# RWKV-7 chunk matrices stored as 64 columns instead of a 128-column block diagonal, in a fused two-block kernel

## The chip, the cores and the metric

The kernel runs on one core of one Trainium2 chip. The metric is the device time of one execution in microseconds (us). The core has a TensorE (PE, matrix products; PEld is its weight load), a VectorE (DVE), a ScalarE (ACT), a GpSimd (POOL) and a SyncE (SP) that issues the DMAs. Each works through its own instructions in a fixed order and waits for the others by semaphores.

## The reference, cut to what matters

A first transformer block (differential and stick-breaking attention, cross attention, an MLP) is followed by a second one: latent attention (MLA) and RWKV-7 side by side, their outputs joined and multiplied by `w_o`, then a product-key expert layer (PEER). The part that changes is RWKV-7: 8 heads of width 64 over 256 tokens, in the reference a recurrence.

```python
def rwkv7_step(state, inp):
    r_t, w_t, k_t, v_t, kk_t, a_t = inp
    sk = jnp.einsum('bhij,bhj->bhi', state, kk_t)
    state = (state * w_t[:, :, None, :]
             - sk[..., None] * (kk_t * a_t)[:, :, None, :]
             + v_t[..., None] * k_t[:, :, None, :])
    y = jnp.einsum('bhij,bhj->bhi', state, r_t)
    return state, y
...
x = x + jnp.concatenate([y_a, y_b], axis=-1) @ w_o[l]   # y_a from MLA, y_b from RWKV-7
x = x + peer_ffn(rms_norm_2(x, g_ffn[l]), w_pq[l], sub_keys[l], expert_u[l], expert_v[l])
```

## The kernel before, in words

RWKV-7 is computed in chunks of 64 tokens. There are four chunks; 128 partitions hold two of them, so an array has an index `t` (which pair) and the two chunks `c` of a pair lie in the partition halves `par(0)` and `par(1)`. The eight heads go in two groups: the generator `r0` does heads 0 to 3, `r1` heads 4 to 7. For each group, pair and head the kernel

- forms the masked chunk matrices AB and KB (products at L1147, in quarters of the PE array; masks on DVE at L1155). AB and KB have 128 columns: both chunks' 64x64 blocks on a diagonal, zeros elsewhere;
- inverts the 16x16 diagonal blocks of a triangular matrix. They go to DRAM and back (L1165, L1167), are inverted on DVE in many small steps (L1176 to L1191), and go out and back again (L1193, L1196) into the zeroed array `p21` that holds Z and X;
- finishes the solve by products of 128x128 matrices with a step on DVE or ACT after each: KB times v (L1214), A0 times X (L1226), Q times Z (L1233), Z times KR (L1242), A0 times Q (L1249), Z times KR again (L1258), which gives KU;
- forms the part of the output that a chunk makes by itself (L1268, L1308), the states from chunk to chunk (L1282, L1285, L1289, then the chain L1299), and adds states times receptance (L1314). The chunk's output is normalised (L1325 to L1336) and written to the tiles `y2[2]` and `y2[3]`.

A float32 product is two MATMUL records in the trace, a float32r product one; so eight records of L1226 are four products.

MLA is the third generator, `mla()`. For each pair of heads it projects queries and keys (L339 to L341), computes scores (L1399, L1400), a softmax on DVE and ACT (L1402 to L1415), transposes (L1421, tiles `me` and `mpT`), outputs (L1432) and their norm (L1435, L1436, L1440), and writes `y2[0]` or `y2[1]` (L676, L677). `w_o` reads all four y2 tiles (L351, L352, L354 and L339 to L341), its weights being split into a high and a low part (`lo`, L332). After it comes `w_pq`, the first product of PEER (tile `xs`).

A scheduler orders the instructions of every engine ahead of time by its own estimates; the code gives priorities:

```python
prio = {r0: R0_PRIO, m_: MLA_PRIO, r1: R1_PRIO}     # 100, 200, 100
...
with tc.high_priority(offset=prio[it]):
    end = next(it, done) is done
```

PSUM has eight banks: `plin()` hands out four (`lin`, used by MLA and the linear layers), `pw(g)` two for each group (`w`).

Of the kernel before, what the change touches and what calls it, by code (L numbers as in the profile page):

```python
# [20 lines left out]
P = 128  # L21
# [17 lines left out]
KB_POOL = 0  # L39
# [86 lines left out]
def _consts():  # L126
# [9 lines left out]
    same = i[:, None] // 64 == i[None, :] // 64  # L136
    items.append(("sT", (same & (i[:, None] < i[None, :])).astype(f)))
    items.append(("iT", (same & (i[:, None] <= i[None, :])).astype(f)))
    for b in (16,):
        m = (i[:, None] // (2 * b) == i[None, :] // (2 * b)) & (i[:, None] // b < i[None, :] // b)  # L140
        items.append((f"m{b}", m.T.astype(f)))
# [74 lines left out]
def body(tc, A, out):  # L216
# [3 lines left out]
    with es:  # L220
# [815 lines left out]
        CDEC = math.exp(-0.5)  # L1036
        rst = ml.tile([P, T], F32, tag="me", name="rst")
# [25 lines left out]
        def rwkv(g):  # L1063
# [72 lines left out]
            yield  # L1136
            if g == 0:
                AB, KB = (st.tile([P, 2, 4, 2, P], F32, name=n) for n in ("AB0", "KB0"))
            else:
                AB, KB = xslot("AB", 2, [2, 4, 2, P])  # L1140
            for dst, lh in ((AB, beta), (KB, khat)):
                for t in range(2):
                    ps = [pw(g), pw(g)]
                    for i in range(2):
                        for pr_, c in ((0, 0), (1, 1), (0, 1), (1, 0)):
                            rs, ts = par(pr_), slice(t * P + c * 64, t * P + c * 64 + 64)
                            PE.matmul(ps[pr_][par(c), i * P:i * P + P].rearrange("p (a s) -> p a s", a=2), lhsT=lh[rs, i, ts],  # L1147
                                      rhs=kr[rs, i, :, ts], start=i == 0, stop=i == 1, skip_group_check=True)
                    for pr_ in range(2):
                        bc = [P, 2, 2, 2, 64]  # L1150
                        o_ = dst[:, t, pr_:4:2].rearrange("p h a (c s) -> p h a c s", c=2)
                        s_ = ps[pr_][:, :T].rearrange("p (h a s) -> p h a s", h=2, a=2)[:, :, :, None].to_broadcast(bc)
                        m_ = m2.rearrange("p a (c s) -> p a c s", c=2)[:, None].to_broadcast(bc)
                        if dst is AB or not KB_POOL:
                            V.tensor_tensor(o_, s_, m_, op=OP.mult)  # L1155
                        else:
                            S.activation(o_, s_, AF.Copy)
                            G.tensor_tensor(o_, o_, m_, op=OP.mult)
                if dst is AB:
# [13 lines left out]
            G.memset(p21, 0.0)  # L1173
# [45 lines left out]
            z4 = lambda p: p.rearrange("p a b (c t) -> p (a b) c t", c=2).rearrange("p a c t -> p (a c) t").rearrange(  # L1219
                "p (t h) s -> p t h s", t=2)  # L1220
            Z, X, Q = z4(p1), z4(p2), z4(p3)
            mk = C("m16")[:, None].to_broadcast([P, 4, P])
            for t in range(2):
                p_ = pw(g)
                for i in range(4):
                    PE.matmul(p_[:, i * P:i * P + P], lhsT=AB[:, t, i, 0], rhs=X[:, t, i], start=i == 0, stop=i == 3,  # L1226
                              skip_group_check=True)
                V.tensor_tensor(Q[:, t], f3(p_), mk, op=OP.mult)
            yield
            for t in range(2):  # L1230
                p_ = pw(g)
                for i in range(4):
                    PE.matmul(p_[:, i * P:i * P + P], lhsT=Q[:, t, i], rhs=Z[:, t, i], start=i == 0, stop=i == 3,  # L1233
                              skip_group_check=True)
                V.tensor_tensor(Z[:, t], Z[:, t], f3(p_), op=OP.subtract)
# [3 lines left out]
            for t in range(2):  # L1239
                p_ = pw(g)  # L1240
                for i in range(4):
                    PE.matmul(p_[:, i * P:i * P + P], lhsT=Z[:, t, i], rhs=KR[:, t, i], start=i == 0, stop=i == 3,  # L1242
                              skip_group_check=True)
                S.activation(Q[:, t], f3(p_), AF.Copy, scale=inv[:, 2:3])
            yield
            for t in range(2):
                p_ = pw(g)
                for i in range(4):
                    PE.matmul(p_[:, i * P:i * P + P], lhsT=AB[:, t, i, 0], rhs=Q[:, t, i], start=i == 0, stop=i == 3,  # L1249
                              skip_group_check=True)  # L1250
                V.scalar_tensor_tensor(hd(KR[:, t]), f3(p_), inv[:, 3:4], hd(KR[:, t]), op0=OP.mult, op1=OP.add)
            yield

            KU = KB[:, :, :, 0].rearrange("p t h (a d) -> p t h a d", a=2)
            for t in range(2):
                p_ = pw(g)
                for i in range(4):
                    PE.matmul(p_[:, i * P:i * P + P], lhsT=Z[:, t, i], rhs=KR[:, t, i], start=i == 0, stop=i == 3,  # L1258
                              skip_group_check=True)
                S.activation(KB[:, t, :, 0], f3(p_), AF.Copy, scale=-1.0)  # L1260
            yield

            rt = kr[:, :, 1]
            p_ = pw(g)
            for t in range(2):
                for h in range(4):
                    o_ = (2 * t + h // 2) * P
                    PE.matmul(p_[par(h), o_:o_ + P], lhsT=KU[:, t, h, 0], rhs=AB[:, t, h, 1], start=t == 0 and h < 2,  # L1268
                              stop=t == 1 and h > 1, skip_group_check=True)
            sj = lambda a: a.rearrange("p j (t s) -> p j t s", t=2)  # L1270
            V.tensor_tensor(sj(rt), p_.rearrange("p (t j s) -> p j t s", t=2, j=2), sj(rt), op=OP.add)
# [7 lines left out]
            for c in (1, 0, 2):  # L1279
                t, cs = c // 2, slice((c % 2) * 64, (c % 2) * 64 + 64)  # L1280
                for rs, o_, h64, h in hh:
                    PE.matmul(pn[c][rs, o_], lhsT=kt[cs, t, h64], rhs=vt[cs, t, h64], start=c < 2 and h < 2, stop=False,  # L1282
                              skip_group_check=True)
                for rs, o_, h64, h in hh:
                    PE.matmul(pn[c][rs, o_], lhsT=bt[cs, t, h64], rhs=KU[cs, t, h, 1], start=False, stop=False,  # L1285
                              skip_group_check=True)
                if c > 0:
                    for rs, o_, h64, h in hh:
                        PE.matmul(pm[c][rs, o_], lhsT=KU[cs, t, h, 0], rhs=bt[cs, t, h64], start=False, stop=False,  # L1289
                                  skip_group_check=True)  # L1290
            ld = lambda c: lend[:, :, c:c + 1].to_broadcast([P, 2, 64])
            V.tensor_tensor(N[:, 0], pj(pn[0]), ld(0), op=OP.mult)
            for c in (1, 2):
                V.tensor_tensor(M[:, c], pj(pm[c]), C("id2")[:, None].to_broadcast([P, 2, 64]), op=OP.add)
            yield
# [7 lines left out]
            p_ = pw(g)  # L1303
            for t in range(2):
                for i in range(2):
                    for h in range(4):
                        rs, o_, h64 = par(h), (2 * t + h // 2) * P, slice(h * 64, h * 64 + 64)
                        PE.matmul(p_[rs, o_:o_ + P], lhsT=KU[:, t, h, 1] if i else vt[:, t, h64],  # L1308
                                  rhs=(AB if i else KB)[:, t, h, 1], start=t + i == 0 and h < 2, stop=False,
                                  skip_group_check=True)  # L1310
            for c in range(1, 4):
                for h in range(4):
                    rs, o_ = par(h), (2 * (c // 2) + h // 2) * P + (c % 2) * 64
                    PE.matmul(p_[rs, o_:o_ + 64], lhsT=N[rs, c - 1, h // 2], rhs=rt[rs, h // 2, c * 64:c * 64 + 64],  # L1314
                              start=False, stop=c == 3 and h > 1, skip_group_check=True)

            Yc, sq, rr_ = p1[:, 0], p1[:, 1], p2[:, 0]
            jt = lambda a: a.rearrange("p j (t s) -> p t j s", t=2)
            pt = p_.rearrange("p (t j s) -> p t j s", t=2, j=2)
# [210 lines left out]
        done = object()  # L1530
# [307 lines left out]
```

## Time and profile before

| | |
|---|---|
| time of 3 runs, us | 1448.38, 1449.96 (median), 1451.75 |
| the profiled execution, us | 1447.91 |
| its span in the trace, us | 1446.1 |
| granted TensorE clock, mean | 0.993 |
| PE busy | 1414.1 us, 98% |
| DVE, ACT, POOL busy | 1087.6, 793.6, 147.3 us |
| second group's block inversion on DVE | 541.6 to 560.0 us |
| second group's first product at L1226 | 569.49 us |
| first product of w_pq | 641.13 us |

The span is what the profiler saw of one execution; 1.8 us lie around it. All positions below are us from the start of the span. RWKV's chunk work and MLA lie between about 500 and 641 us; what stands before and behind that is the same program in both kernels.

### The profile page before, as it was taken

The numbers are of one execution on the slowest core, as the hardware profiler recorded it, in microseconds if no ns is written. First come the engines' busy times: TensorE is split into PE (matmuls) and PEld (weight loads), VectorE is DVE, ScalarE is ACT, GpSimd is POOL, SyncE is SP. The second block draws the span as 40 slices with busy tenths as digits, with TensorE's granted clock in tenths as the row PEclk, the third lists the DMA queues.
The fourth block names the chain that finished last, engine by engine and source line by source line (L and its number), as shares of the span: only waits on it lengthen the run. The fifth ranks groups of instructions, "written<-read, shape, count | busy, mean of one in ns | idle before, by whom it ended". The sixth has DMA issues, their size and how long they took to land.

```text
span 1446.1 us, 24458 instructions
## 1 busy us (share of the span) xinstructions
PE 1414.1 (98%) x9262; PEld 1248.9 (86%) x9262; DVE 1087.6 (75%) x1986; ACT 793.6 (55%) x1334; POOL 147.3 (10%) x159
## 2 busy tenths in 40 slices
PE   8999999999999888999999999999999999999998
PEld 7888999888888866899999988888888888888887
DVE  7876676886659988579999789899996555555554
ACT  6856655555557445554545566555555444444443
POOL 6500101000114443220000000000000000000000
PEclk9999999999999998999999999999999999999999
DMA  6543445566664411155565555556556566666664
GB/s 220 176 149 104 142 146 155 183 190 201 197 197 148 144 45 27 38 150 190 162 189 175 178 180 158 170 152 176 157 175 199 191 191 195 195 190 193 197 192 146
DMA packets 75911, 237.36 MB, mean 164 GB/s; under 512 B 14608, under 2 KB 17808, under 8 KB 75792
## 3 DMA queue, kind: packets, MB, share of 16 engines
q1 hardware_dynamic: 75792, 235.79, 53.1%
q8 instruction: 73, 1.20, 0.3%
q14 instruction: 46, 0.38, 0.1%
HBM read 233.27 MB, written 2.49 MB: 163 GB/s over the span
## 4 chain that ended last, share of the span: by engine, by line
PE 89%; DVE 7%; DMA 2%; ACT 1%; issue 1%; SPq 0%; DVEq 0%; ACTq 0%
PE lin L348 19%; PE lin L354 17%; PE w L1818 8%; PE w L1815 8%; PE w L1814 8%; PE lin L351 7%; PE lin L352 7%; PE w L1725 2%; DVE lo L332 2%; PE lin L500 1%; PE lin L502 1%; PE lin L501 1%; PE w L1639 0%; ACT hi L330 0%; DMA raw<-w_o 0%
## 5 line engine op out<-in xcount | busy, mean ns | idle before, releaser
L332 DVE TENSOR_TENSOR lo<-raw,hi 128x1024 fp32r<-128x1024 f32 (+1 forms) x432 | 530.7, 1229 | 249.1 <-PE w L1815 92.2
L330 ACT ACTIVATE hi<-raw 128x1024 fp32r<-128x1024 f32 x437 | 458.9, 1050 | 408.9 <-DMA raw<-eu 112.6
L1815 PE MATMUL w<-lo,wh 128*128 128x512 f32 x504 | 155.3, 389 | 0.0
L1818 PE MATMUL w<-hi,wl 128*128 128x512 f32 x504 | 155.2, 389 | 0.0
L348 PE MATMUL lin<-hbh,hi 128*128 128x512 f32 x344 | 135.5, 394 | 0.0
L348 PE MATMUL lin<-hbl,hi 128*128 128x512 f32 x344 | 135.1, 393 | 0.0
L1814 PE MATMUL w<-hi,wh 128*128 128x512 f32 x504 | 134.8, 389 | 0.0
L354 PE MATMUL lin<-hbh,lo 128*128 128x256 f32 x512 | 129.7, 286 | 0.7 <-DVE lo L332 0.7
L354 PE MATMUL lin<-hbl,lo 128*128 128x256 f32 x512 | 127.9, 283 | 0.0
L1818 PEld LDWEIGHTS w<-hi,wl 128*128 128x128 f32 x504 | 94.6, 188 | 19.7
L1814 PEld LDWEIGHTS w<-hi,wh 128*128 128x128 f32 x504 | 94.5, 188 | 19.6
L1815 PEld LDWEIGHTS w<-lo,wh 128*128 128x128 f32 x504 | 94.5, 188 | 19.5
L354 PEld LDWEIGHTS lin<-hbh,lo 128*128 128x128 f32 x512 | 97.3, 190 | 3.5 <-DVE lo L332 1.1
L354 PEld LDWEIGHTS lin<-hbl,lo 128*128 128x128 f32 x512 | 97.7, 191 | 2.6
L1797 ACT ACTIVATE wh<-GA 128x512 fp32r<-128x512 f32 x64 | 40.5, 634 | 73.8 <-PE w L1815 73.8
L348 PEld LDWEIGHTS lin<-hbl,hi 128*128 128x128 f32 x344 | 64.9, 189 | 10.9
L348 PEld LDWEIGHTS lin<-hbh,hi 128*128 128x128 f32 x344 | 64.9, 189 | 10.6
L546 POOL TENSOR_TENSOR sqa<-sqa,sq 128x256 f32<-128x256 f32 x37 | 34.9, 945 | 314.6 <-ACT sq L542 299.8
L348 PE MATMUL lin<-a,hi 128*128 128x512 f32 x256 | 64.8, 395 | 0.0
L348 PE MATMUL lin<-xs,hi 128*128 128x512 f32 x256 | 63.3, 392 | 0.0
L354 PE MATMUL lin<-xs,lo 128*128 128x256 f32 x384 | 53.8, 285 | 0.0
L348 PEld LDWEIGHTS lin<-xs,hi 128*128 128x128 f32 x256 | 46.4, 189 | 8.5
(597 smaller groups left out, 3073.8 us busy)
## 6 DMA issues: line engine op xcount, KB each, us to landing
raw<-eu SPq DMA_DIRECT2D x128, 512.0 KB, 3.7
raw<-ev SPq DMA_DIRECT2D x128, 512.0 KB, 4.2
raw<-w_up SPq DMA_DIRECT2D x32, 512.0 KB, 3.6
raw<-w_down SPq DMA_DIRECT2D x32, 512.0 KB, 4.5
raw<-w_in SPq DMA_DIRECT2D x20, 512.0 KB, 3.7
raw<-w_in_s SPq DMA_DIRECT2D x16, 512.0 KB, 4.9
raw<-w_pq SPq DMA_DIRECT2D x16, 512.0 KB, 3.6
raw<-w_in_m SPq DMA_DIRECT2D x8, 512.0 KB, 3.7
```

Of the source, the lines that this page charges most:

```text
L330: S.activation(hi[:, :n], raw[:, :n], AF.Copy)
L332: eng.tensor_tensor(lo[:, :n], raw[:, :n], hi.bitcast(F32)[:, :n], op=OP.subtract)
L348: PE.matmul(ps.rearrange("p (a t) -> p a t", a=2), lhsT=wh[:, o], rhs=x.both[:, c], start=at, stop=False, skip_group_check=True)
L351: PE.matmul(ps[:, :T], lhsT=wh[:, o], rhs=x[0][:, c], start=at, stop=False, skip_group_check=True)
L352: PE.matmul(ps[:, :T], lhsT=wh[:, o], rhs=x[1][:, c], start=False, stop=False, skip_group_check=True)
L354: PE.matmul(ps[:, :T], lhsT=wl[:, o], rhs=x[0][:, c], start=False, stop=stop and c == ks[-1][0], skip_group_check=True)
L546: G.tensor_tensor(self.acc, self.acc, q, op=OP.add)
L1725: PE.matmul(p_[:, o_:o_ + P], lhsT=first[:, i], rhs=parts[s][:, i], start=i % 4 == 0 and s == 0, stop=i % 4 == 3 and s == 1, skip_group_ch ...
L1797: S.activation(wh_, w2, AF.Copy)
L1814: PE.matmul(acc[t][d], lhsT=wh_[:, i, ts], rhs=vh[:, ds], start=c + i == 0, stop=False, skip_group_check=True)
L1815: PE.matmul(acc[t][d], lhsT=wh_[:, i, ts], rhs=vl[:, ds], start=False, stop=False, skip_group_check=True)
L1818: PE.matmul(acc[t][d], lhsT=wl_[:, i, ts], rhs=vh[:, ds], start=False, stop=False, skip_group_check=True)
```

## The change

The two chunks of a pair keep their 64x64 blocks under each other, in 64 columns, instead of on a diagonal of 128. The masks at L1155 write half as many elements, the array to be zeroed is half as large (one `p1` for X and Z instead of `p21`), and KU gets an array of its own (`p2`). Every product of 128x128 matrices becomes two products of 64 rows by 64, one for each chunk, in two opposite quarters of the PE array; `chunks()` issues them, both into one PSUM bank, in different partitions. The states' accumulators move from `pw(g)` to `plin()` banks, and the states of odd and even chunks are issued in turn. The outputs that a chunk makes by itself are issued ahead of the chain of states, into two `pw(g)` banks, one for each chunk of a pair; they too are quarter products now. What follows them is cut along chunks, not pairs.

```diff
             if g == 0:
-                AB, KB = (st.tile([P, 2, 4, 2, P], F32, name=n) for n in ("AB0", "KB0"))
+                AB, KB = (st.tile([P, 2, 4, 2, 64], F32, name=n) for n in ("AB0", "KB0"))
...
-                        bc = [P, 2, 2, 2, 64]
-                        o_ = dst[:, t, pr_:4:2].rearrange("p h a (c s) -> p h a c s", c=2)
...
-                        if dst is AB or not KB_POOL:
-                            V.tensor_tensor(o_, s_, m_, op=OP.mult)
...
+                        V.tensor_tensor(dst[:, t, pr_:4:2], ps[pr_][:, :T].rearrange("p (h a s) -> p h a s", h=2, a=2),
+                                        m2[:, None].to_broadcast([P, 2, 2, 64]), op=OP.mult)
...
-            G.memset(p21, 0.0)
+            ZX = fl(p1.rearrange("p a b t -> p (a b) t")).rearrange("p (z a s) -> p z a s", z=2, a=8)
+            G.memset(p1, 0.0)
...
-                    PE.matmul(p_[:, (4 * t + h) * 64:(4 * t + h + 1) * 64], lhsT=KB[:, t, h, 0],
-                              rhs=vt[:, t, h * 64:h * 64 + 64], start=t + h == 0, stop=t + h == 4,
-                              skip_group_check=True)
+                    for c in range(2):
+                        PE.matmul(p_[par(c), (4 * t + h) * 64:(4 * t + h + 1) * 64], lhsT=KB[par(c), t, h, 0],
+                                  rhs=vt[par(c), t, h * 64:h * 64 + 64], start=t + h == 0, stop=t + h == 4,
+                                  skip_group_check=True)
...
+            def chunks(t, lh, rh, n=64):
+
                 p_ = pw(g)
                 for i in range(4):
-                    PE.matmul(p_[:, i * P:i * P + P], lhsT=AB[:, t, i, 0], rhs=X[:, t, i], start=i == 0, stop=i == 3,
-                              skip_group_check=True)
-                V.tensor_tensor(Q[:, t], f3(p_), mk, op=OP.mult)
-            yield
+                    for c in range(2):
+                        PE.matmul(p_[par(c), i * n:i * n + n], lhsT=lh[par(c), t, i], rhs=rh[par(c), t, i], start=i == 0,
+                                  stop=i == 3, skip_group_check=True)
+                return p_
...
+                V.tensor_tensor(Q1[:, t], s4(chunks(t, A0, X)), mk, op=OP.mult)
...
+                V.tensor_tensor(Z[:, t], Z[:, t], s4(chunks(t, Q1, Z)), op=OP.subtract)
...
+                S.activation(Q[:, t], f3(chunks(t, Z, KR, P)), AF.Copy, scale=inv[:, 2:3])
...
+                S.activation(hd(KU[:, t]), f3(chunks(t, Z, KR, P)), AF.Copy, scale=-1.0)
...
-            pa, pb = pw(g), pw(g)
+            pa, pb = plin(), plin()
...
+            rows_ = [states(1), chain(states, (0, 2))]
+            while rows_:
+                rows_ = [r_ for r_ in rows_ if [next(r_, done) for _ in range(2)][-1] is not done]
+
+
+            rt = kr[:, :, 1]
+            po = [pw(g), pw(g)]
+            for i in range(3):
+                for t in range(2):
+                    for h in range(4):
+                        o_ = (i < 2) * T + (2 * t + h // 2) * 64
+                        for c in range(2):
+                            PE.matmul(po[c][par(h), o_:o_ + 64],
+                                      lhsT=KU[par(c), t, h, 2 - i] if i else vt[par(c), t, h * 64:h * 64 + 64],
+                                      rhs=(AB if i else KB)[par(c), t, h, 1], start=i + t == 0 and h < 2,
+                                      stop=i + t == 3 and h > 1, skip_group_check=True)
...
-            p_ = pw(g)
-            for t in range(2):
-                for i in range(2):
-                    for h in range(4):
-                        rs, o_, h64 = par(h), (2 * t + h // 2) * P, slice(h * 64, h * 64 + 64)
-                        PE.matmul(p_[rs, o_:o_ + P], lhsT=KU[:, t, h, 1] if i else vt[:, t, h64],
-                                  rhs=(AB if i else KB)[:, t, h, 1], start=t + i == 0 and h < 2, stop=False,
-                                  skip_group_check=True)
```

The scheduler orders the changed program anew. Two places matter below. The first is the row in which DVE starts the block inversion of `r0` (`p_4977`; `AB_5957` is the matrix of `r1`, `kg` and `n` belong to MLA). Before:

```order
L1176 TENSOR_SCALAR p_4977<-p_4977 64x8
L1183 TENSOR_TENSOR p_4977<-p_4977 64x8
L1462 TENSOR_TENSOR ksq_5953<-lin_6229,rk_4890 64x512
L1183 TENSOR_TENSOR p_4977<-p_4977 64x8 x3
L1155 TENSOR_TENSOR AB_5957<-w_5970,cst 128x2x256
L1155 TENSOR_TENSOR KB_5812<-w_5860,cst 128x2x256
L1155 TENSOR_TENSOR KB_5812<-w_5861,cst 128x2x256
L517 SCALAR_TENSOR_TENSOR n_1055_6097<-n_1056_6098,n_1055_6097 128x512
L1185 TENSOR_REDUCE t_1017_5874<-p_4977 64x16
L1155 TENSOR_TENSOR AB_5957<-w_5971,cst 128x2x256
L1155 TENSOR_TENSOR AB_5957<-w_6054,cst 128x2x256
```

After:

```order
L515 SCALAR_TENSOR_TENSOR n_1055_6113<-n_1056_6114,n_1055_6113 128x512
L1386 TENSOR_TENSOR kg_6121<-kgu_5954,n_1055_6113 128x512
L1171 TENSOR_SCALAR p_4977<-p_4977 64x8
L1178 TENSOR_TENSOR p_4977<-p_4977 64x8 x4
L1180 TENSOR_REDUCE t_1017_5874<-p_4977 64x16
L1183 TENSOR_TENSOR p_4977<-p_4977,t_1017_5874 64x8 x4
L1185 TENSOR_REDUCE p_4977<-p_4977 64x2x2 x4
L1178 TENSOR_TENSOR p_4977<-p_4977 64x64
L1454 TENSOR_TENSOR ksq_5953<-lin_6269,rk_4890 64x512
L1178 TENSOR_TENSOR p_4977<-p_4977 64x64
L1151 TENSOR_TENSOR AB_5957<-w_5970,cst 128x2x128
L1151 TENSOR_TENSOR AB_5957<-w_5971,cst 128x2x128
```

The masks are half as wide, the `n` and `kg` steps of MLA now stand ahead of the inversion, and its small steps follow each other with less between them.

The second place is the row of PE around the last scores of MLA (`kg_6805` before, `kg_6953` after; `w_...` tiles are RWKV's, `lin_...` those of MLA, of `w_o` and, after the change, of RWKV's states). Before:

```order
L1399 MATMUL lin_6892<-kg_6805,qg_6693 128x128
L1400 MATMUL lin_6892<-kg_6805,qg_6693 128x256
L1400 MATMUL lin_6877<-kg_6805,qg_6693 128x256
L1282 MATMUL w_6382<-tk_5270 64x64 x2
L1285 MATMUL w_6382<-KB_5812,tk_5270 64x64 x4
L1289 MATMUL w_6382<-tk_5270,KB_5812 64x64
L1258 MATMUL w_6576<-KR_5781,p_4990 128x128
L1268 MATMUL w_6624<-AB_5957 64x128
L1436 MATMUL lin_6862<-sq_6867,cst 128x256
L1268 MATMUL w_6624<-AB_5957 64x128 x3
```

After:

```order
L1391 MATMUL lin_7025<-kg_6953,qg_6858 128x128
L1391 MATMUL lin_7040<-kg_6953,qg_6858 128x128
L1392 MATMUL lin_7040<-kg_6953,qg_6858 128x256
L1392 MATMUL lin_7025<-kg_6953,qg_6858 128x256
L1424 MATMUL lin_7010<-mpT_7008,mv_5917 64x256
L1424 MATMUL lin_7010<-mpT_6989,mv_5918 64x128
L1424 MATMUL lin_7010<-mpT_7008,mv_5918 64x128
L1323 MATMUL w_6955<-p_4990,cst 128x256
L1428 MATMUL lin_7010<-sq_7015,cst 128x256
L1413 MATMUL lin_7055<-ident,me_7030 128x128 x3
L1413 MATMUL lin_7061<-ident,me_7045 128x128 x3
L1424 MATMUL lin_7067<-mpT_7059,mv_5917 64x256
```

Before, RWKV's products for both groups follow the last scores, and `w_o` comes later. After, RWKV's products all stand ahead of the last scores; behind them stand MLA's own last steps, the norms of RWKV (L1323, L1331 before) and `w_o` (L349, L350).

## Rows read from the trace of the kernel before

**Rows 1.** Page of the kernel before, its parts 1 and 4.

```profile
PE 1414.1 (98%) x9262; PEld 1248.9 (86%) x9262; DVE 1087.6 (75%) x1986; ACT 793.6 (55%) x1334; POOL 147.3 (10%) x159
...
PE 89%; DVE 7%; DMA 2%; ACT 1%; issue 1%; SPq 0%; DVEq 0%; ACTq 0%
```

**Rows 2.** Busy time by stretch: us, PE, PEld, DVE, ACT, POOL (x instructions), granted clock.

```profile
540.00:550.00 10.00, 3.04 (x18) 2.07 (x18) 9.95 (x41) 3.85 (x12) 9.53 (x7) 0.75 0.01 3
550.00:560.00 10.00, 9.18 (x42) 7.69 (x43) 9.97 (x25) 2.74 (x6) 0.28 (x1) 0.56 0.15 23
```

**Rows 3.** Chain of waits, 518 to 563 us: start, us, what.

```profile
518.61 1.30 DVE AB L1155 x2
...
526.36 2.19 DMA p<-blk_in
528.57 0.18 DVE p L1176
...
559.74 0.29 DVE p L1191
...
560.30 2.16 DMA blk_out<-p
...
563.15 2.02 PE w L1226 x16
```

**Rows 4.** DVE in order of time, 508 to 561 us: start, us, what.

```profile
511.58 0.41 DVE L514 TENSOR_SCALAR am<-w 128x256 f32<-128x256 f32 x1
...
530.29 1.27 DVE L1155 TENSOR_TENSOR KB<-w,cst 128x512 f32<-128x512 f32 x2
531.49 1.47 DVE L517 SCALAR_TENSOR_TENSOR n<-n,n 128x512 f32<-128x512 f32 x1
...
534.24 0.67 DVE L1394 TENSOR_TENSOR kg<-kgu,n 128x512 f32<-128x512 f32 x1
...
558.54 1.21 DVE L332 TENSOR_TENSOR lo<-raw,hi 128x1024 fp32r<-128x1024 f32 x1
...
568.12 0.69 DVE L1235 TENSOR_TENSOR p<-p,w 128x512 f32<-128x512 f32 x1 [0.21 <-DMA p<-blk_out]
```

**Rows 5.** PE in order of time, behind its long wait and at at L1226 of r1.

```profile
550.82 0.90 PE L1421 MATMUL lin<-ident,me 128*128 128x128 f32 x3 [6.46 <-DVE me L1415]
...
569.49 1.06 PE L1226 MATMUL w<-p,AB 128*128 128x128 f32 x8
```

**Rows 6.** PE by line and form, 505 to 642 us.

```profile
L1214 PE MATMUL w<-tk,KB 128*128 128x64 f32 x16 | 2.0, 278 | 0.0
```

**Rows 7.** PE in order of time: rows that price 64-row products.

```profile
603.10 0.45 PE L1282 MATMUL w<-tk 64*64 64x64 f32 x8
...
615.54 0.66 PE L1308 MATMUL w<-AB,tk 128*64 128x128 f32 x8
...
617.44 0.91 PE L1314 MATMUL w<-kr,h 64*64 64x64 f32 x24
```

**Rows 8.** PE, products of 128 columns in quarters.

```profile
515.48 0.65 PE L1147 MATMUL w<-kr,p 64*64 64x128 f32 x12
```

**Rows 9.** PE, last MLA scores to the first products of w_pq.

```profile
596.76 1.03 PE L1400 MATMUL lin<-kg,qg 128*128 128x256 f32 x4
...
603.59 0.33 PE L1421 MATMUL lin<-ident,me 128*128 128x128 f32 x1
...
610.05 0.70 PE L1436 MATMUL lin<-sq,cst 128*128 128x256 f32 x2
...
638.16 1.21 PE L354 MATMUL lin<-y2h,lo 128*128 128x256 f32 x8 [0.93 <-DVE lo L332]
...
641.13 0.28 PE L351 MATMUL lin<-xs,hi 128*128 128x256 f32 x1
```

**Rows 10.** ACT in order of time, end of the last MLA chain.

```profile
608.35 0.38 ACT L1435 ACTIVATE sq<-lin 128x256 f32<-128x256 f32 x1 [2.08 <-PE lin L1432]
...
612.26 0.42 ACT L676 ACTIVATE y2h<-myo 128x256 fp32r<-128x256 f32 x1
```

More of the change, by code (lines that the diff above doesn't have):

```diff
@@ L38 @@
 B_POOL = 0
-KB_POOL = 0
 X_W = 6
@@ L135, in _consts @@
     items.append(("bones", (i[:, None] // 64 == i[None, :] // 64).astype(f)))
[L136 to L141, printed above, removed]
+    k, j = i[:, None] % 64, np.arange(64)[None, :]
+    items.append(("sT", (k < j).astype(f)))
+    items.append(("iT", (k <= j).astype(f)))
+    items.append(("m16", ((k // 32 == j // 32) & (j // 16 < k // 16)).astype(f)))
     items.append(("id2", (i[:, None] % 64 == np.arange(64)[None, :]).astype(f)))
@@ L1217, in rwkv @@
             S.activation(KR[:, :, :, 1], p_.rearrange("p (t h d) -> p t h d", t=2, h=4), AF.Copy)
             yield
[L1219 to L1222, printed above, removed]
-            for t in range(2):
+            X, Z = (ZX[:, z].rearrange("p (t h) s -> p t h s", t=2) for z in range(2))
@@ L1239, in rwkv @@
             for t in range(2):
[L1240 to L1244, printed above, removed]
+                S.activation(Q[:, t], f3(chunks(t, Z, KR, P)), AF.Copy, scale=inv[:, 2:3])
             yield
             for t in range(2):
[L1247 to L1251, printed above, removed]
+                V.scalar_tensor_tensor(hd(KR[:, t]), f3(chunks(t, A0, Q, P)), inv[:, 3:4], hd(KR[:, t]), op0=OP.mult, op1=OP.add)
             yield
-            KU = KB[:, :, :, 0].rearrange("p t h (a d) -> p t h a d", a=2)
+            KU = p2.rearrange("p a b t -> p (a b t)").rearrange("p (t h a d) -> p t h a d", t=2, h=4, a=2)
             for t in range(2):
[L1256 to L1260, printed above, removed]
-            yield
-            rt = kr[:, :, 1]
-            p_ = pw(g)
-            for t in range(2):
-                for h in range(4):
[L1267 to L1271, printed above, removed]
+                S.activation(hd(KU[:, t]), f3(chunks(t, Z, KR, P)), AF.Copy, scale=-1.0)
+            yield
             mn = lambda a: fl(a)[:, :3 * P].rearrange("p (c j d) -> p c j d", c=3, j=2)
@@ L1275, in rwkv, with states @@
             pj = lambda p: p.rearrange("p (j d) -> p j d", j=2)
-            pa, pb = pw(g), pw(g)
+            pa, pb = plin(), plin()
             pn, pm = (pa[:, 0:P], pb[:, 0:P], pa[:, P:2 * P]), (None, pb[:, P:2 * P], pa[:, 2 * P:3 * P])
             hh = [(par(h), slice((h // 2) * 64, (h // 2) * 64 + 64), slice(h * 64, h * 64 + 64), h) for h in range(4)]
-            for c in (1, 0, 2):
-                t, cs = c // 2, slice((c % 2) * 64, (c % 2) * 64 + 64)
+            def states(c):
+                t, cs = c // 2, par(c)
@@ L1281, in rwkv @@
                 for rs, o_, h64, h in hh:
-                    PE.matmul(pn[c][rs, o_], lhsT=kt[cs, t, h64], rhs=vt[cs, t, h64], start=c < 2 and h < 2, stop=False,
-                              skip_group_check=True)
+                    yield PE.matmul(pn[c][rs, o_], lhsT=kt[cs, t, h64], rhs=vt[cs, t, h64], start=c < 2 and h < 2, stop=False,
+                                    skip_group_check=True)
                 for rs, o_, h64, h in hh:
-                    PE.matmul(pn[c][rs, o_], lhsT=bt[cs, t, h64], rhs=KU[cs, t, h, 1], start=False, stop=False,
-                              skip_group_check=True)
+                    yield PE.matmul(pn[c][rs, o_], lhsT=bt[cs, t, h64], rhs=KU[cs, t, h, 1], start=False, stop=False,
+                                    skip_group_check=True)
@@ new lines, in rwkv @@
+            rt = kr[:, :, 1]
+            po = [pw(g), pw(g)]
+            for i in range(3):
+                for t in range(2):
+                    for h in range(4):
[5 more added lines that the diff above has]
+                                      stop=i + t == 3 and h > 1, skip_group_check=True)
@@ L1291, in rwkv @@
+            ch = lambda a, c: a.rearrange("p j (t c s) -> p t j c s", t=2, c=2)[:, :, :, c]
+            pt = lambda p: p.rearrange("p (t j s) -> p t j s", t=2, j=2)
             ld = lambda c: lend[:, :, c:c + 1].to_broadcast([P, 2, 64])
@@ L1294, in rwkv @@
                 V.tensor_tensor(M[:, c], pj(pm[c]), C("id2")[:, None].to_broadcast([P, 2, 64]), op=OP.add)
+            for c in range(2):
+                V.tensor_tensor(ch(rt, c), pt(po[c][:, :T]), ch(rt, c), op=OP.add)
             yield
@@ L1301, in rwkv @@
                 V.tensor_tensor(N[:, c], pj(pn[c]), ld(c), op=OP.mult)
-            p_ = pw(g)
-            for t in range(2):
-                for i in range(2):
-                    for h in range(4):
-                        rs, o_, h64 = par(h), (2 * t + h // 2) * P, slice(h * 64, h * 64 + 64)
-                        PE.matmul(p_[rs, o_:o_ + P], lhsT=KU[:, t, h, 1] if i else vt[:, t, h64],
-                                  rhs=(AB if i else KB)[:, t, h, 1], start=t + i == 0 and h < 2, stop=False,
-                                  skip_group_check=True)
             for c in range(1, 4):
                 for h in range(4):
-                    rs, o_ = par(h), (2 * (c // 2) + h // 2) * P + (c % 2) * 64
-                    PE.matmul(p_[rs, o_:o_ + 64], lhsT=N[rs, c - 1, h // 2], rhs=rt[rs, h // 2, c * 64:c * 64 + 64],
-                              start=False, stop=c == 3 and h > 1, skip_group_check=True)
+                    rs, o_ = par(h), T + (2 * (c // 2) + h // 2) * 64
+                    PE.matmul(po[c % 2][rs, o_:o_ + 64], lhsT=N[rs, c - 1, h // 2], rhs=rt[rs, h // 2, c * 64:c * 64 + 64],
+                              start=False, stop=c > 1 and h > 1, skip_group_check=True)
             Yc, sq, rr_ = p1[:, 0], p1[:, 1], p2[:, 0]
-            jt = lambda a: a.rearrange("p j (t s) -> p t j s", t=2)
-            pt = p_.rearrange("p (t j s) -> p t j s", t=2, j=2)
             for p, y_ in zip("hl", y2):
@@ L1323, in rwkv @@
             cuts = [slice(i, i + 1) for i in range(2)] if g in TAIL_CUT else [slice(0, 2)]
-            for i in cuts:
-                S.activation(jt(sq)[:, :, i], pt[:, :, i], AF.Square)
-                V.tensor_tensor(jt(Yc)[:, :, i], pt[:, :, i], jt(gt[g])[:, :, i], op=OP.mult)
+            for c in range(2):
+                S.activation(ch(sq, c), pt(po[c][:, T:]), AF.Square)
+                V.tensor_tensor(ch(Yc, c), pt(po[c][:, T:]), ch(gt[g], c), op=OP.mult)
             yield
```

31 lines of the change are left out of this document (15 added, 16 removed).

## The prediction

> **What bounds the kernel now.** The page comes first: PE is busy for 98% of the span and is 89% of the chain that ended last [rows 1]. Over the whole span a product saved is time saved. But that is a mean, and the change touches only 500 to 641 us. So I read the busy times by stretch [rows 2]. There PE has one hole: it is busy for 3.04 of the 10 us from 540 to 550, while DVE is busy for 9.95. Right behind it, from 550 to 560, PE is busy again, but the granted clock is 0.56. The chain of waits says why [rows 3]: it goes from the masks of AB over the DMAs to DRAM and back to the block inversion on DVE, which is followed by another trip to DRAM. DVE works without a pause from 528.57 to 560.0. PE's 6.46 us wait ends with a softmax step of MLA (`me`) that stood in the same DVE queue [rows 5].
>
> So the stretch falls in two. Up to about 563 us DVE and the DMAs set the pace, and PE products cost nothing. From 569.49, the first product of `r1` (X), to the first product of `w_pq` at 641.13 [rows 5, 9], PE sets it, with one wait of 0.93 us for a split of weights [rows 9].
>
> **What the change does to DVE.** A mask of 128x512 takes 1.27 us for two that follow each other, with 0.67 to 0.68 for one alone; a 128x256 step from PSUM takes 0.41 [rows 4]. I take 0.26 off each. Sixteen masks are run, eight of them between the inversion's start and the end of `r1`'s: 8 x 0.26 = 2.1 us less. In the new order the steps L517 (1.47) and L1394 (0.6, by the spacing of like steps) have moved ahead of the inversion, where DVE waited for the DMA and where the other eight masks give 2.1 back: 2.0 less. The split L332 (1.21) moves behind it: 1.2 less. Two masks stand ahead of the first DMA: 0.5. The inversion of `r1`, which ended at 560.0 [rows 3], then ends at 560.0 - 5.8 = 554.2. What was late there is not late next: the trip to DRAM is unchanged. It took from 560.0 to 568.1, where DVE stops waiting for it [rows 4], so 8.1 us, and X of `r1` can start at 562.3, 7.2 earlier.
>
> **What it does to PE.** I take starts as the price, since records overlap.
> - L1226 and L1233: 64 records at 0.112 (eight in 1.06, the last of which alone would show 0.28) [rows 5] become 128 records of 64 columns in quarters, at 0.030 as in L1314 (24 in 0.91) [rows 7]: 7.2 to 3.9, 3.3 less.
> - L1242, L1249, L1258: 96 records at 0.112 become 192 quarters of 128 columns. The nearest row is L1147, 12 in 0.65 with four quarters in use [rows 8], so (0.65 - 0.27)/11 = 0.035. Only two quarters are used here, and half the array costs 0.055 for as many columns in L1308 (8 in 0.66) [rows 7]. Between these I take 0.045: 10.8 to 8.6, 2.2 less. The bounds are 4.1 less, 0.2 less, and, if two quarters can't run side by side, 0.112 each: 10.7 more.
> - KB times v (L1214), 32 records at 0.112 (2.0 busy for 16 is the overlapped sum) [rows 6] to 64 at 0.030: 1.7 less, counted as nothing, since it lies ahead of PE's wait. Without that cover it would be 1.7.
> - Own outputs: 96 records at 0.055 become 192; states: 128 records at 0.031 (eight in 0.45) [rows 7], now in turn between the two halves. Both use all four quarters. Half of L1147's 0.035 is 0.018, L1314's 0.030 the other bound: at 0.024, 5.3 + 4.0 becomes 4.6 + 3.1, 1.6 less (bounds 3.5 less, 0.3 more).
>
> The changes between products of the whole array and of quarters number 86 before and 90 after, counted in the two orders: nothing. Smaller POOL and ACT steps run beside DVE's and PE's and count as nothing too. PE's work falls by 3.3 + 2.2 + 1.6 = **7.1 us**.
>
> **What becomes of PE's waits.** This decides the sum.
> - The hole at 540 to 550: the softmax step that ends it comes earlier by the 2.1 of the masks and the 2.0 of the moved steps, less 0.6 for a second `n` step that has moved ahead of it: 3.5 less.
> - A new hole ahead of X of `r1`: PE resumes at 550.8 - 3.5 = 547.3. In the new order fewer rows stand between there and X; priced row by row they last 11.5 us, until 558.8. X waits for its DMA until 562.3: 3.5 more.
> - The end: the wait of 0.93 for the split of weights goes, since DVE is free by then: 0.9 less.
> - The tail of MLA. Before, from the end of the last scores (597.8) to the end of `y2h` (612.68) [rows 9, 10] passed 14.9 us, and PE filled them with RWKV products. ACT's square ended at 608.73 and its norm product started at 610.05 [rows 9, 10]: 1.3 of it was queueing, and about one more at the transposes, so the chain itself needs 12.6. After, all of RWKV's products stand ahead of these scores. The states hold `lin` banks, and MLA's last projection stands behind them in PE's order. What is left to fill the chain (transposes, outputs, two norms of RWKV, twelve products of `w_o`) comes to 5.1 at these prices: 7.5 us of idle PE, which is new.
>
> Idle time: -3.5 + 3.5 - 0.9 + 7.5 = +6.6. **Sum**: 6.6 - 7.1 = -0.5. The low clock behind the old hole cost 9.18 x (1 - 0.56) = 4.0 us [rows 2]. The new kernel has two or three shorter holes in place of a long one. Whether the clock falls behind each, no row shows; the bounds are 4.0 less and 4.0 more, and I take no change. The profiled execution took 1447.91, so 1447.4; that one lies 2.05 below the median of the three, so **1449.5** against 1449.96.
>
> As a second way to the same number: with X at 562.3 and the new order priced row by row, the last scores end at about 607; 12.6 more for the chain and 180 products of `w_o` at 0.12 put `w_pq` at 641.2, against 641.13.
>
> **The rivals.**
> - *Forecast: the gain is spent in the tail.* -0.5, 1446 to 1453. Chance 0.45.
> - *The gain stays.* If PE's order and MLA's readiness agree better than I price them (own products at 0.018, scores ending by 601), RWKV's last evictions and norms cover the tail but for 1 us: -7.1 - 3.5 + 3.5 - 0.9 + 1 = -7.0, so 1443. For it speaks that the inversion gets 5.8 us shorter; against it that the order shows no RWKV product behind the scores. Chance 0.29.
> - *Slower by the tail.* The `lin` banks: with two held by each group's states from early on, MLA's projections have two or none left, and the last scores slip. From 607.5 on for their end the kernel is slower. At 610, with the clock low behind the tail's idle stretch for a further 2, it is +5: 1455. Chance 0.17.
> - *Quarters in one bank take turns.* `chunks()` writes both quarters into one bank. Then the three 128-column products cost 10.7 more, and X and Z gain nothing: -0.5 + 2.2 + 10.7 + 3.3 = +15.7, so 1465.5. L1314 speaks against it: its quarters write one bank at 0.030 a record. Chance 0.04. The Trainium skill (TensorEngine Tiling (Array Packing), Restrictions and Gotchas, Gotcha 1) says that different row tiles can't access the same PSUM bank simultaneously; by that rule this rival would be the outcome, and the trace of L1314 does not agree.
> - *Nothing changes*, since what DVE saves returns as waiting for DMA: 1450. Chance 0.05.
>
> **How the numbers follow.** This kernel's runs tell a change of 0.2%, 2.9 us, from none. The forecast's own spread gives 0.31 to "same", 0.09 to faster, 0.05 to slower. With the rivals: faster 0.09 + 0.28 = 0.37, slower 0.05 + 0.16 + 0.04 = 0.25, same 0.38. The range leaves out the turn-taking and the far ends of both neighbours: 1442 to 1455.5; the forecast's own is 1446 to 1453.
>
> **What would show it.** Right: masks at 0.41; the second inversion ending near 554; X of `r1` near 562 behind a PE wait for the DMA; L1227 at 0.030 a record for 64 columns and 0.045 for 128; some 7 us of PE waits for DVE and ACT between 607 and 620; `w_pq` near 641. Wrong: quarters spaced 0.11 apart; last scores before 602 or after 610; a granted clock below 1 where `w_o` starts; PE waiting for `lin` banks between 570 and 600.

## The result and the profile after

The changed kernel took 1467.68 us (median; 1465.86 to 1469.96), the kernel before 1449.17 on the same chip: a ratio of 1.0121, with a 95% interval of 1.0099 to 1.0143. It is slower by about 17.5 us, outside the range. The profiled execution took 1465.86, its span is 1464.1.

The page of the changed kernel, parts 1 and 4, which answer to [rows 1]:

```profile
PE 1420.5 (97%) x9550; PEld 1249.2 (85%) x9550; DVE 1084.1 (74%) x1989; ACT 795.6 (54%) x1335; POOL 145.2 (10%) x159
...
PE 86%; DVE 8%; DMA 2%; ACT 1%; issue 1%; SPq 1%; POOL 0%; DVEq 0%; ACTq 0%; POOLq 0%
```

The page shows little: PE has 6 us more of busy time and one point less of the span. The busy times by stretch of 5 us (columns as in [rows 2], and behind the clock the busy share of the DMA engines and GB/s) show where the time went:

```profile
545.00:550.00 5.00, 1.84 (x10) 1.87 (x10) 4.97 (x25) 2.64 (x8) 2.59 (x3) 0.50 0.26 33
550.00:555.00 5.00, 5.00 (x46) 3.32 (x48) 4.49 (x14) 1.51 (x6) 0.00 (x0) 0.50 0.07 7
555.00:560.00 5.00, 5.00 (x33) 4.17 (x31) 0.85 (x2) 0.38 (x1) 0.00 (x0) 0.50 0.24 42
...
580.00:585.00 5.00, 3.89 (x50) 3.75 (x51) 2.75 (x9) 1.57 (x5) 0.00 (x0) 0.69 0.01 3
...
600.00:605.00 5.00, 2.42 (x97) 2.10 (x95) 4.41 (x11) 3.43 (x8) 1.28 (x1) 1.00 0.35 107
605.00:610.00 5.00, 4.92 (x33) 3.40 (x33) 2.45 (x6) 3.90 (x10) 2.77 (x3) 0.66 0.19 78
610.00:615.00 5.00, 4.02 (x66) 3.16 (x65) 4.88 (x17) 3.13 (x10) 1.05 (x1) 0.76 0.17 43
...
620.00:625.00 5.00, 0.74 (x3) 0.30 (x2) 4.96 (x18) 4.51 (x14) 0.00 (x0) 0.78 0.00 0
625.00:630.00 5.00, 3.91 (x15) 2.67 (x16) 1.36 (x7) 2.74 (x8) 0.00 (x0) 0.53 0.00 0
630.00:635.00 5.00, 2.55 (x17) 1.62 (x16) 0.72 (x2) 1.69 (x4) 0.00 (x0) 1.00 0.00 0
635.00:640.00 5.00, 5.00 (x29) 4.84 (x29) 1.14 (x2) 1.27 (x2) 0.00 (x0) 0.66 0.19 32
```

In the kernel before, the granted clock was 1.00 in every such stretch from 560 on; four of them:

```profile
580.00:585.00 5.00, 5.00 (x46) 4.95 (x44) 4.79 (x10) 4.55 (x10) 2.64 (x1) 1.00 0.37 125
605.00:610.00 5.00, 5.00 (x90) 4.36 (x88) 0.58 (x2) 1.36 (x3) 0.00 (x0) 1.00 0.29 52
620.00:625.00 5.00, 5.00 (x42) 4.92 (x40) 4.06 (x6) 2.25 (x6) 1.99 (x2) 1.00 0.42 113
635.00:640.00 5.00, 4.07 (x34) 3.86 (x33) 3.87 (x6) 3.71 (x8) 2.32 (x2) 1.00 0.18 43
```

In the changed kernel it falls again at 580, 605, 625 and 635, each time at or behind holes in PE's work (0.50 is the lower of its two levels, 1.2 of 2.4 GHz; values between are stretches with both). And PE does 0.74 us of work in the five from 620. The longest waits of PE from 560 to 660 us (engine, line, who ended the wait; us in total, times, longest):

```profile
PE lin L1413 <- DVE me L1407: 4.8, 1, 4.8
PE lin L1382 <- ACT ksq L1456: 2.7, 1, 2.7
PE lin L349 <- ACT y2h L674: 2.0, 1, 2.0
PE lin L1428 <- ACT sq L1427: 1.0, 2, 0.5
PE w L1308 <- DVE kr L1296: 1.0, 1, 1.0
PE lin L1262 <- ACT me L1400: 1.0, 1, 1.0
```

The first four are steps of MLA's last heads. The last, at 580.71, is a state product of RWKV that waits until MLA's softmax has read a `lin` bank. The kernel before had two waits from 560 to 645:

```profile
PE lin L354 <- DVE lo L332: 0.9, 1, 0.9
PE w L1226 <- DMA blk_out<-p: 0.7, 1, 0.7
```

PE of the changed kernel in order of time, the rows that answer to [rows 5] and [rows 9]:

```profile
548.16 0.87 PE L1413 MATMUL lin<-ident,me 128*128 128x128 f32 x3 [5.85 <-DVE me L1407]
...
563.59 0.29 PE L1227 MATMUL w<-p,AB 64*64 64x64 f32 x2 [0.63 <-DMA p<-blk_out]
...
617.59 1.03 PE L1392 MATMUL lin<-kg,qg 128*128 128x256 f32 x4
...
626.09 1.66 PE L1413 MATMUL lin<-ident,me 128*128 128x128 f32 x6 [4.80 <-DVE me L1407]
...
634.78 0.51 PE L349 MATMUL lin<-y2h,hi 128*128 128x256 f32 x2 [1.98 <-ACT y2h L674]
...
659.38 0.28 PE L349 MATMUL lin<-xs,hi 128*128 128x256 f32 x1
```

X of `r1` starts at 563.59, 5.9 us earlier than before. But MLA's last scores end at 618.62 instead of 597.79, and `w_pq` starts at 659.38 instead of 641.13: 18.25 us later, which is the whole difference of the spans (18.0).

What put the scores there is seen in the products of the states. Each row has the shortest, median and longest duration in ns, then the first and last start (the changed kernel's L1262, then L1282 of the kernel before):

```profile
L1262 PE MATMUL lin<-tk x48: 216/289/366, 550.5 to 591.5; 64*64 64x64 f32 x48
```

```profile
L1282 PE MATMUL w<-tk x48: 218/218/267, 595.2 to 606.4; 64*64 64x64 f32 x48
```

These products (keys times values) need nothing of the solve. In `pw(g)` banks, which the solve uses too, the first came at 595.2. In `lin` banks they did not have to wait for the solve, and the first came at 550.5, 45 us earlier. From then on the states of `r0` hold two of the four `lin` banks, and from 580.7 and 582.6 those of `r1` the other two; `r0` gives its two back by about 593, and `r1` keeps its two until its chain ends (the last L1301 starts at 600.9). (Which banks are whose is read from the code; the trace shows only `lin`.) MLA, which needs these banks, made no projection (L337 to L339) between 567.9 and 594.1: the next one starts when `r0` has given its banks back.

### The profile page after: what moved, and what is told of

Read it like the earlier page. It is cut to its first block, busy times and chain, and to the rows that moved or that the text cites. A ratio compares the mean times of both kernels' runs of the same rounds, so it can differ in the third digit from the quotient of the medians.

```text
span 1464.1 us, 25037 instructions
## 1 busy us (share of the span) xinstructions
PE 1420.5 (97%) x9550; PEld 1249.2 (85%) x9550; DVE 1084.1 (74%) x1989; ACT 795.6 (54%) x1335; POOL 145.2 (10%) x159
## 4 chain that ended last, share of the span: by engine, by line
PE 86%; DVE 8%; DMA 2%; ACT 1%; issue 1%; SPq 1%; POOL 0%; DVEq 0%; ACTq 0%; POOLq 0%
PE lin L346 19%; PE lin L352 17%; PE w L1805 8%; PE w L1806 8%; PE w L1809 8%; PE lin L349 7%; PE lin L350 7%; PE w L1716 2%; DVE lo L330 1%; PE lin L498 1%; PE lin L500 1%; PE lin L499 1%; PE w L1227 1%; DMA raw<-w_xq 1%; PE w L1630 0%
```

## The experiments

Times are ratios to the kernel before on the same chip, with 95% intervals. The table has for each profiled execution the end of MLA's last scores, the start of `w_pq`, and from 500 us to there the idle time of PE and what the granted clock took, both summed over stretches of 5 us (idle: length less busy; clock: busy time times one less the clock). The time given under each run is its median.

| kernel | ratio | scores end | w_pq | PE idle | clock |
|---|---|---|---|---|---|
| before | 1 | 597.8 | 641.1 | 12.2 | 6.9 |
| after | 1.0121 [1.0099, 1.0143] | 618.6 | 659.4 | 23.9 | 19.9 |
| states_w_banks | 1.0055 [1.0035, 1.0074] | 595.3 | 648.0 | 18.0 | 10.7 |
| own_behind_only | 1.0133 [1.0108, 1.0158] | 624.5 | 665.6 | 26.9 | 21.9 |
| before_lin_states | 1.0198 [1.0169, 1.0227] | 635.9 | 674.3 | 28.6 | 20.4 |
| mla_two_steps | 1.0030 [1.0017, 1.0044] | 602.9 | 649.9 | 17.3 | 12.8 |
| w_banks_r0_150 | 1.0001 [0.9986, 1.0015] | 594.2 | 642.0 | 11.3 | 7.6 |
| w_banks_r0_300 | 0.9990 [0.9976, 1.0004] | 598.4 | 637.6 | 11.3 | 6.8 |
| w_banks_r1_0 | 1.0048 [1.0032, 1.0063] | 596.7 | 651.0 | 15.9 | 12.8 |
| w_banks_cuts4 | 1.0055 [1.0034, 1.0075] | 596.1 | 646.1 | 17.1 | 9.1 |
| before_r0_300 | 1.0017 [1.0001, 1.0032] | 601.5 | 641.7 | 12.9 | 6.2 |
| lin_r0_300 | 1.0047 [1.0031, 1.0063] | 614.2 | 651.1 | 19.0 | 14.3 |
| w_banks_300_200 | 1.0115 [1.0096, 1.0134] | 622.9 | 659.7 | 16.2 | 23.3 |
| w_banks_300_pre3 | 0.9998 [0.9986, 1.0010] | 599.7 | 639.7 | 11.7 | 7.9 |

**Which part of the change costs it.** The theory (A) is that the states in `lin` banks push MLA's last scores behind all of RWKV's products, so that nothing is left to cover MLA's last softmax. The rivals: quarter products cost more than priced (B); the own outputs ahead of the chain do it (C).

*states_w_banks.* The states go back to `pw(g)`; for want of banks the own outputs and their DVE step go behind the chain.

```diff
-            pa, pb = plin(), plin()
+            pa, pb = pw(g), pw(g)
...
-            rt = kr[:, :, 1]
-            po = [pw(g), pw(g)]
-            for i in range(3):
...
             for c in range(1, 3):
                 for rs, o_, h64, h in hh:
...
+            rt = kr[:, :, 1]
+            po = [pw(g), pw(g)]
+            for i in range(3):
```

> The changed kernel with the states' accumulators back in the pw(g) banks; these two banks are then taken until the chain of states is done, so the outputs that a chunk makes by itself come behind the chain, as in the kernel before. 64-column matrices and quarter products stay. If the lin banks are what put MLA's last scores behind RWKV's work (theory A), the last scores end near 600 instead of 618.6, w_o follows without the 4.8 us wait, w_pq starts near 636 to 641, and the time is 1442 to 1449. If quarter products or their clock are what costs (theory B), the last scores may move but w_pq stays near 660 and the time is 1462 to 1468. If the own outputs ahead of the chain cost it (theory C), the result is as under A, and the run with only the own outputs moved tells C from A.

Measured: 1457.81 us, ratio 1.0055. The first state product starts at 593.4, as late as before, the scores end at 595.3 as theory A has it, and a good half of the loss is gone. `w_pq` at 648.0 is later than expected; what is left is the subject of the next set.

*own_behind_only.* The same move of the own outputs, with the states left in `lin` banks.

> The changed kernel with only the own outputs moved behind the chain of states; the states stay in the lin banks. Theory A (lin banks): the last scores stay behind all of RWKV's products, near 618, and the time stays at 1464 to 1469. Theory C (own outputs ahead): the last scores end near 600 and the time falls below 1452. Theory B (quarters): 1464 to 1469 too, so this run is read together with the one with the states in the pw(g) banks.

Measured: 1470.96 us, ratio 1.0133, scores at 624.5. Theory C falls: with the own outputs behind the chain and the banks as in the change, nothing is won.

*before_lin_states.* One line of the kernel before, all of its matrices still 128 columns wide:

```diff
-            pa, pb = pw(g), pw(g)
+            pa, pb = plin(), plin()
```

> The kernel before, block-diagonal 128 columns throughout, with one line changed: the states' accumulators in lin banks. Theory A: MLA's last scores move behind RWKV's products (from 597.8 to about 609), the softmax of the last heads leaves PE without work, and the time rises by 8 to 18 us, to 1457 to 1467. Theories B and C: no change beyond 3 us, 1447 to 1452.

Measured: 1480.5 us, ratio 1.0198. This line alone costs about 29 us, more than the whole change and more than theory A had expected. PE in order of time, then PE's waits from 540 to 675 us:

```profile
633.98 1.90 PE L1400 MATMUL lin<-kg,qg 128*128 128x256 f32 x4
```

```profile
PE lin L1421 <- DVE me L1415: 14.0, 3, 6.4
PE w L1331 <- ACT p L1325: 3.4, 1, 3.4
PE w L1226 <- DMA p<-blk_out: 2.1, 1, 2.1
```

MLA's last scores come 38 us later than before. Its softmax steps (`me`) leave PE idle for 14.0 us, of which 6.4 is the hole ahead of 560 that the kernel before has too (6.46 [rows 5]). The other 7.6, from 560 on, are new:

```profile
PE lin L1421 <- DVE me L1415: 7.6, 2, 5.4
```

Theory A stands, and theory B can't explain this kernel, which has no new quarter product.

*mla_two_steps.* The changed kernel, with MLA taken two steps further in each round instead of one.

```diff
-MLA_STEPS = 1
+MLA_STEPS = 2
```

> The changed kernel with one number changed: MLA's generator is advanced by two steps a round, so that its last heads are emitted sooner. The states stay in the lin banks. The order of PE then has about 124 rows of RWKV behind the last scores, against 1. Theory A in the form that the missing cover behind the last scores is the cost: 1450 to 1458, the last scores near 610 and less than 2 us of wait behind them. Theory B: 1462 to 1468.

Measured: 1454.85 us, ratio 1.0030, as expected in size: the states stay in the `lin` banks, MLA goes ahead, and the scores end at 602.9. The wait behind them goes, but another of 4.3 us appears, for an output of RWKV (`y2h`, L1327).

**What is left once the states are back.** With the states in `pw(g)` banks PE's longest wait behind the scores is this one (states_w_banks, PE and ACT in order of time, then two stretches):

```profile
624.17 0.79 PE L349 MATMUL lin<-y2h,hi 128*128 128x256 f32 x2 [5.55 <-ACT y2h L1327]
```

```profile
623.49 0.63 ACT L1327 ACTIVATE y2h<-p 128x512 fp32r<-128x512 f32 x1 [2.50 <-DVE p L1326]
```

```profile
620.00:625.00 5.00, 0.83 (x3) 0.60 (x3) 4.84 (x7) 2.00 (x5) 2.90 (x2) 0.82 0.00 0
625.00:630.00 5.00, 5.00 (x24) 5.00 (x25) 1.14 (x2) 1.05 (x2) 0.00 (x0) 0.50 0.15 25
```

The low clock, 0.82 and then 0.50, stands at and behind this wait. The 128x512 write is the output of `r0`, which `w_o` needs first. It ends at 624.1, behind part of the output of `r1`: both groups come to their last norms together. In the kernel before, those of `r0` were 8 us ahead. Theory D: this step is the rest of the loss. The four kernels that follow are states_w_banks with one more number changed.

```diff
-R0_PRIO = 100
+R0_PRIO = 150
```

> States in the pw(g) banks as before, and the first group's priority raised from 100 to 150, so that its tail no longer runs in step with the second group's. Theory D (in the kernel with the states in the pw(g) banks, what is left over the kernel before is that both groups' last norms come at once and w_o has nothing to work on meanwhile): the 5.6 us wait of w_o for the first group's output goes, and with it the low clock behind it (about 3): 1444 to 1450. If quarter products cost the rest (theory B): 1454 to 1459.

Measured: 1449.49 us, ratio 1.0001. The wait is gone, and so is the low clock behind it:

```profile
620.00:625.00 5.00, 5.00 (x49) 4.88 (x46) 2.74 (x5) 3.24 (x6) 1.10 (x1) 1.00 0.69 201
625.00:630.00 5.00, 5.00 (x43) 4.95 (x42) 2.83 (x5) 2.38 (x5) 0.19 (x1) 1.00 0.64 194
```

```diff
-R0_PRIO = 100
+R0_PRIO = 300
```

> The same with a priority of 300, above MLA's 200. Theory D: the first group's outputs are ready before MLA's last ones, w_o is fed; but the last scores slip by some 5 us of PE work against 150: 1444 to 1452. Theory B: 1454 to 1460.

Measured: 1446.45 us, ratio 0.9990; `w_pq` starts at 637.6, 3.5 us earlier than before. The stretches (now of 20 us) have a clock of 1.00 throughout:

```profile
580.00:600.00 20.00, 19.26 (x261) 14.72 (x259) 16.92 (x43) 14.70 (x36) 7.29 (x6) 1.00 0.24 68
600.00:620.00 20.00, 19.17 (x295) 16.36 (x294) 9.73 (x25) 9.62 (x23) 1.34 (x2) 1.00 0.18 50
620.00:640.00 20.00, 18.51 (x149) 17.93 (x148) 14.79 (x25) 12.58 (x26) 6.98 (x5) 1.00 0.52 157
```

```diff
-R1_PRIO = 100
+R1_PRIO = 0
```

> States in the pw(g) banks, the second group's priority lowered from 100 to 0, the first left at 100. Theory D: the groups are taken apart the other way, by a later second group: 1443 to 1450, or up to 1455 if its tail then comes so late that w_o is done with the rest before. Theory B: 1454 to 1460.

Measured: 1456.73 us, ratio 1.0048: a miss by 2 us of the upper end. The groups are apart, but now the tail of `r1` comes too late: `w_o` waits for it 1.3 us, and other waits of RWKV's chain (2.8 for DVE's KR step) lie open.

```diff
-CUTS_O = (6, 8)
+CUTS_O = (4, 8)
```

> States in the pw(g) banks, priorities as in the change; only w_o is cut after four parts of its inputs (MLA's) rather than six, so that 72 of its products need nothing from RWKV. The two groups stay in step. Theory D: the wait of w_o is covered by these products: 1446 to 1452, with the wait below 2 us. Theory B: 1454 to 1460.

Measured: 1455.97 us, ratio 1.0055: a miss. The 72 products that need MLA alone were not enough; the wait for `y2h` of L1327 is still 4.8 us. Of these four kernels only those that keep the groups apart remove it.

**Controls.** *before_r0_300*: the kernel before with the same `R0_PRIO = 300`.

> The kernel before (128 columns, states in pw(g) banks) with the first group's priority at 300: a control for the run with the same priority on 64 columns. If the priority alone gives what that run gained, this one comes out at 0.997 to 1.000 of the kernel before; if 64 columns give it, this one is at 1.000 to 1.008, since its order leaves fewer RWKV products (83 rows against 149) behind MLA's last scores.

Measured: 1450.76 us, ratio 1.0017 [1.0001, 1.0032]. So a priority of 300 by itself gives nothing with 128 columns; with 64 columns the ratio was 0.9990, lower by 0.3%, on another chip. Against the kernel before itself neither shows a gain, and the kernel before was not run with 150.

*lin_r0_300*: the changed kernel with `R0_PRIO = 300`, states in `lin` banks.

> The changed kernel, states in the lin banks, with the first group's priority at 300. Theory A: priorities don't cure what the banks do, since the second group's states still hold lin banks ahead of MLA's last projection: 1458 to 1470. Against A: 1444 to 1452, as with the states in the pw(g) banks.

Measured: 1455.84 us, ratio 1.0047: between the two expectations. The priority mends some 11 of the 17.5 us though the banks stay; the scores end at 614.2. So the banks act through the order, and the order can be bent back in part by other means.

*w_banks_300_200*: states in `pw(g)` banks, but

```diff
-R0_PRIO = 100
+R0_PRIO = 300
...
-R1_PRIO = 100
+R1_PRIO = 200
```

> States in the pw(g) banks, priorities 300 and 200 for the two groups, MLA at 200. The last scores have 41 rows of RWKV behind them, against 118 with 300 and 100. If cover behind the last scores is what counts, this is slower than that run by 2 to 8: 1448 to 1455.

Measured: 1465.33 us, ratio 1.0115, far more than expected. It says that the banks are not needed for the loss: take the second group up to MLA's priority and the first above it, and the scores end at 622.9 and the time is that of the changed kernel. By the table more of this loss is clock (23.3 against 6.9 before) than idle time (16.2 against 12.2):

```profile
600.00:605.00 5.00, 3.39 (x42) 3.23 (x44) 4.22 (x10) 3.30 (x7) 1.28 (x1) 0.63 0.01 2
605.00:610.00 5.00, 5.00 (x36) 3.25 (x36) 0.88 (x4) 2.62 (x6) 0.00 (x0) 0.50 0.22 77
```

*w_banks_300_pre3*: w_banks_r0_300 with `PRE0 = 3` instead of 2.

> States in the pw(g) banks, priority 300 for the first group, which is also taken one step further before the rounds with MLA begin. The order has 123 rows behind the last scores and they end 0.5 us of PE work earlier. Expected 1443 to 1449, the best candidate for a version ahead of both kernels; if it is not below the kernel before by its interval, the 64 columns gain no more than 3 us here.

Measured: 1448.82 us, ratio 0.9998. The best version found is w_banks_r0_300; it beats the changed kernel by 1.3%, and the kernel before by 0.1% with an interval that takes in no change.

## Why the prediction was wrong

**PE's work was right in sum.** X and Z cost 0.0305 us a record (20 in 0.80), as taken. The three products of 128 columns cost 0.055 (16 in 1.09), not the 0.045 taken: 1.9 us too hopeful. The own outputs cost 0.0156 (80 in 1.45), not 0.024: 1.6 too careful. The rows, all PE of the changed kernel in order of time:

```profile
564.49 0.80 PE L1227 MATMUL w<-p,AB 64*64 64x64 f32 x20
...
570.10 1.09 PE L1227 MATMUL w<-KR,p 64*64 64x128 f32 x16 [0.45 <-DVE p L1236]
...
600.98 1.45 PE L1285 MATMUL w<-AB,p 64*64 64x64 f32 x80
```

So the rival of quarters taking turns in one bank is out: L1227 writes both quarters into one bank, and yet their records start in pairs: 0.007 us between the two, and 0.058 (64 columns) or 0.109 (128) from pair to pair. (The rival's sum, -0.5 + 2.2 + 10.7 + 3.3 = 15.7, gives 1465.7, not 1465.5.)

**DVE was right.** A mask takes 0.41 for one and 0.74 for two; the inversion of `r1` ends at 554.5 (predicted 554.2), PE's first wait ends at 548.16 (predicted 547.3), and X starts at 563.59 (predicted 562.3):

```profile
536.82 0.74 DVE L1151 TENSOR_TENSOR AB<-w,cst 128x256 f32<-128x256 f32 x2
...
554.12 0.37 DVE L1186 COPY p<-p 64x256 f32<-64x256 f32 x1
```

The hole that was forecast ahead of X (3.5 us) was 0.63: PE reached X late, because it ran at a clock of 0.50 from 545 to 560.

**The step that failed is "with X at 562.3 and the new order priced row by row, the last scores end at about 607", with its "I take no change" for the clock.** The scores ended at 618.6. Of these 11.6 us, 1.3 is X; waits that the pricing did not have account for 5.4 (0.45 + 0.40 + 0.95 + 2.66 + 0.98, for MLA's own `ksq` and `me` and for RWKV's steps); a lower clock between 563 and 619 for about 5, summed over stretches as in the table. I had priced rows that stand in a queue and taken for granted that each is ready when its turn comes. In the changed order it was not: MLA's last projection, with its norm, scores and softmax, stood at the end, a chain of steps on several engines with little beside it. In the terms of the sum: the idle time of +6.6 was +11.7, and the clock, put at nothing, was +13.0. Three of the signs of being wrong came: the last scores after 610, a granted clock below 1 where `w_o` starts (0.53 from 625), and the wait of a state product for a `lin` bank (0.95 at 580.71).

**The tail of MLA** was the right idea with the wrong size. From the end of the scores to the end of `y2h` (634.73) it took 16.1 us, not 12.6: the norms of RWKV stand ahead of the softmax steps on DVE (busy 4.96 of the 5 us from 620). PE's idle time in it, 0.55 + 4.80 + 0.47 + 1.98 = 7.8, is near the 7.5 forecast; of the 8.4 us of work beside it 4.6 stand in the two stretches at 0.78 and 0.53. From there `w_o` took 24.6, not 21.6, with the clock at 0.66 in one stretch, the wait for a split of weights that was to go (0.9), and two shorter ones (0.5 together). Together 11.6 + 3.5 + 3.0 = 18.1: the miss against 641.2.

**The clock** cost 19.9 us in all against 6.9: 13.0 more, where I had bounds of 4 either way. That and the idle time, 11.7 more instead of 6.6, come to 24.7; less the 18.25 by which `w_pq` is later, some 6.4 is left for the work that PE saved, near the 7.1 forecast. The figures are rough, since a stretch has one mean clock. The two parts lie apart: ahead of 565, where DVE and the DMAs set the pace, the clock took 4.8 more and the idle time was 2.1 less; behind 565 the idle time was 13.8 more and the clock took 8.2.

**The rival "slower by the tail" had the mechanism**: the `lin` banks. Its size was taken at 5 us, and its chance at 0.17. That the states would start 45 us earlier, and `lin` banks so be held for 50 us, first by `r0` and then by `r1`, stood in the new order of PE, which has state products ahead of X; I used these rows for their price, not for what they hold.

What stays open: why the clock fell behind holes of 1 us here (580 to 585, PE busy 3.89 of 5, 0.69) and not in the kernel before, which has a like stretch at 635 (busy 4.07, 1.00). No run separates that.

## What to carry to other kernels

When an accumulator moves to another pool of banks, ask two things of the new order: when its first product can start there, and who else draws on that pool from then until it is read out. A saving of 7 us in a nearly full engine is worth nothing if the order that comes with it takes the cover from the longest chain of small steps: look at what stands behind that chain's last product, in every order, and price its steps as a chain, not as work. And keep two like streams out of step if they end in the same consumer.

## What the runs showed of the hardware

- Products in two opposite quarters of the array ran side by side, though they write one bank. Counted from start to start, for 128 columns a record took 0.112 us on the whole array [rows 5], 0.055 with two halves [rows 7] and 0.055 with two opposite quarters; for 64 columns it took 0.112 on the whole array too (L1214 [rows 6]), 0.0305 with two quarters into one bank and 0.0156 with four into two banks. At 128 columns two opposite quarters therefore win nothing over halves. The change makes two records out of one, so its products of 128 columns gain nothing over the whole array either (2 x 0.055 against 0.112), while X and Z, which go from 128 columns to 64, take 2 x 0.0305 = 0.061 instead of 0.112. The Trainium skill (TensorEngine Tiling (Array Packing), Gotcha 1) says that different row tiles can't access one bank at once; the 20 records in 0.80 us do not bear that out for disjoint partitions.
- The granted clock was lost behind short holes too. From 580 to 640 six stretches of 5 us ran at 0.53 to 0.78, at or behind waits of 0.4 to 4.8 us; the kernel before, with no wait over 0.93 there, ran at 1.00 throughout. Behind 565 this took 8.2 us, beside 13.8 us more of idle time.
